# Narrow levels and diagonal of a gated linear attention multiplied in blocks of 32 keys and collected in a small tile of their own

## The chip, the cores and the metric

The kernel runs on one core of a Trainium2 chip. The metric is device time in microseconds (us) of one execution, as the median over several executions. Each executed kernel also has one profiled execution, which left a page of sums and a trace of every instruction; TensorE is called PE in it, its weight loads PEld, VectorE DVE, ScalarE ACT, GpSimd POOL, and SyncE, which starts the transfers, SP.

## What is computed

The program is one encoder block: an RMSNorm, a mix of two attention branches (stick-breaking attention and gated linear attention, GLA), and a gated MLP with a causal convolution, for 528 tokens of width 1024 in fp32 (16 learned tokens ahead of 512). The change touches only the GLA branch. It has four heads with keys of 128 channels and values of 256:

```python
def _gla(q, k, v, g):                     # S_t = diag(exp(g_t)) S_{t-1} + k_t^T v_t,  o_t = q_t S_t
    ...
        cum = jnp.cumsum(gi, axis=2)
        diff = cum[:, :, :, None, :] - cum[:, :, None, :, :]
        decay = jnp.exp(jnp.where(causal[None, None, :, :, None], diff, -jnp.inf))
        att = jnp.einsum('bhtd,bhsd,bhtsd->bhts', qi, ki, decay)
        o = jnp.einsum('bhts,bhsv->bhtv', att, vi) + jnp.einsum('bhtd,bhdv->bhtv', qi * jnp.exp(cum), state)
```

Inside a chunk, `att[t,s]` is a sum over channels d of q[t,d] k[s,d] exp(cum[t,d] - cum[s,d]) for s up to t. The decay depends on the channel, so the sum isn't one matrix product of q and k.

## The kernel before

The kernel works on chunks of 128 tokens: four, and a last one of 16 (`CHUNKS`). The function `gla` (L426) handles one head and builds the transposed attention of every chunk in one tile, `attT` (128 keys on the partitions, 528 queries along the row: chunk by chunk a block of 128 by 128, then 16 by 16).

To make matrix products of it, it splits the causal triangle of a chunk by levels. For a level lv, a chunk falls into pieces of 2 lv tokens; the queries of the second half of a piece see the keys of its first half. For these pairs exp(cum[t]-cum[s]) is split at the last key of the first half into a factor for the query and one for the key. `factors` (L441) makes them: DVE subtracts (`D`, L447), ACT takes two exponentials (L448, L449), DVE multiplies the keys (`kt`, L455) and the queries (`qt`, L456; only the query halves are kept, so a chunk has 64 columns at every level). `kt` is one of two buffers that are used in turn; where no keys of the level stand, it holds zeros or keys of an earlier level, whose products are unwanted. `D` has two buffers, too.

- The **wide levels** 64 and 32 multiply piece by piece (L466): 4 products of 64 keys by 64 queries, and 8 of 32 keys by 32. The products of level 32 go in turn to partitions 0 and 64 of the result `pl`. ACT copies the results to their places in `attT` (L469).
- The **narrow levels** 16, 8, 4, 2 and 1 (`LEVELS`, L470 on) multiply a whole chunk: 128 keys by the chunk's 64 queries (L476), four products for a level; levels 8 and less add one product of 16 keys by 8 queries for the last chunk (L478). Nearly all of a result is unwanted, since only pairs in the same piece count. A predicated copy of DVE (L481) writes those where a mask is set into `attT`: 128 x 256 elements for a level, and 16 x 8 for the tail. The masks `mk` (128 x 264 each) are made once, early in the program: POOL fills and selects 64 columns, and 8 for the tail (L341 to L354), and DVE copies the 64 columns three times.
- The **diagonal** (a token with itself; the factor is 1) is a product of k and q themselves, 128 x 128 for each chunk and 16 x 16 for the last (L437), into a tile `dg` from the pool of large results (`mmt`). A predicated copy of 128 x 512 (L439) puts the diagonal into `attT`, with a mask `mkd`.

Then `attT` is split into two tiles of fewer bits, `ah` and `al` (L484 to L486), which the output products read. `vt` (L497) are transposes of the values, `cum` (L430) the products that make the cumulated gates, `kdt` transposes of the keys for the state.

On PE an fp32 product is issued as two instructions, so that 4 products of L476 stand in the trace as x8. An fp32r product, as in the projections, is one.

The order of the work isn't the one in which the code stands. A scheduler plays the program through with estimated durations and writes one instruction stream for each engine. The heads run one after the other (L575 to L577): `gla(h)` and, beside it, projections that need nothing of it: the next head's `gla_proj` (keys, queries, values) and the gates `gr` of the same head (L555). Their products (L110: 128 x 128 weights by 256 or 258 columns) fill PE's stream between the small products of `gla`. They are called fills below. Their weights are brought by SP's queue, cast by ACT to `wh` (L89), and the rest `wl` is made by POOL (L90).

Small results lie in a pool `pss` (L65) with two tags of two buffers each: `pst(name)` takes tag "s", `pst(name, "z")` tag "z", which the levels use. Large results lie in `psm` with two buffers (`mmt`).

Of the kernel before, what the change touches and what calls it, by code (L numbers as in the profile page):

```python
# [9 lines left out]
F32 = mybir.dt.float32  # L10
F32R = mybir.dt.float32r
I32 = mybir.dt.int32
AF = mybir.ActivationFunctionType
ALU = mybir.AluOpType
PSUM = bass.MemoryType.PSUM

P = 128
# [4 lines left out]
T = NM + SEQ  # L22
# [18 lines left out]
CHUNKS = [(0, 128), (128, 128), (256, 128), (384, 128), (512, 16)]  # L41
# [3 lines left out]
CUT = (8, 16)  # L45
EARLY = 3
WIDE, LEVELS = (64, 32), (16, 8, 4, 2, 1)


@with_exitstack  # L50
def block_kernel(ctx: ExitStack, tc: tile.TileContext, x, meta_tokens, norm_mix_pre, w_in, w_gk_up, b_gk,
# [3 lines left out]
    pe, act, dve, pool, sp = nc.tensor, nc.scalar, nc.vector, nc.gpsimd, nc.sync  # L55

    x = x[0]
    out = out[0]
# [110 lines left out]
    ident = cst.tile([P, P], F32, name="ident")  # L169
# [45 lines left out]
    with tc.tile_pool(name="p0", bufs=2, side="right") as p0:  # L215
# [80 lines left out]
        for t, src in ((ghT, gla_head_norm[0]), (g1T, norm_mix_post[0]), (g2T, norm_ffn_pre[0]), (mT, meta_tokens[T0:, :])):  # L296
            n = src.shape[0] // P if len(src.shape) == 1 else src.shape[0] * KT
            r = p0.tile([n, P], F32, name=f"small{len(small)}", bufs=1)
# [34 lines left out]
    with ExitStack() as pgs:  # L333
        pgc = pgs.enter_context(tc.tile_pool(name="pgc", bufs=1))

        mk = {}
        mkd = pgc.tile([P, T], F32, name="mkd")
        for h in LEVELS:
            with tc.issue_after(low4.ins) if h < EASY else ExitStack():
                m = pgc.tile([P, 264], F32, name=f"mk{h}")  # L340
                pool.memset(m, 1.0)  # L341
                v3 = m[:, :64].rearrange("p (b i) -> p b i", i=h)
                pool.affine_select(out=v3, in_=v3, compare_op=ALU.is_ge, fill=0.0, base=0,
                                   pattern=[[-2 * h, 64 // h], [0, h]], channel_multiplier=1)
                pool.affine_select(out=v3, in_=v3, compare_op=ALU.is_ge, fill=0.0, base=h - 1,
                                   pattern=[[2 * h, 64 // h], [0, h]], channel_multiplier=-1)
                if h <= 8:
                    vt = m[:, 256:264].rearrange("p (b i) -> p b i", i=h)
                    pool.affine_select(out=vt, in_=vt, compare_op=ALU.is_ge, fill=0.0, base=0,
                                       pattern=[[-2 * h, 8 // h], [0, h]], channel_multiplier=1)  # L350
                    pool.affine_select(out=vt, in_=vt, compare_op=ALU.is_ge, fill=0.0, base=h - 1,
                                       pattern=[[2 * h, 8 // h], [0, h]], channel_multiplier=-1)
                with tc.issue_after(last_yg[0].ins):
                    dve.tensor_copy(m[:, 64:256].rearrange("p (c t) -> p c t", c=3), m[:, :64].unsqueeze(1).broadcast_to([P, 3, 64]))  # L354
                mk[h] = m
        with ExitStack():
            pool.memset(mkd, 1.0)
            pool.affine_select(out=mkd[:, 512:], in_=mkd[:, 512:], compare_op=ALU.is_equal, fill=0.0, base=0,
                               pattern=[[-1, 16]], channel_multiplier=1)
        with tc.issue_after(last_yg[0].ins):  # L360
            dve.tensor_copy(mkd[:, :512].rearrange("p (c t) -> p c t", c=4), ident.unsqueeze(1).broadcast_to([P, 4, P]))


        G = pgc.tile([P, 5, 512], F32, name="G")
# [61 lines left out]
        def gla(h, k, q, vT):  # L426

            pt = mmt(f"cum{h}")
# [3 lines left out]
            act.copy(cum, pt[:, :T])  # L432
            attT = pg.tile([P, T], F32, tag="attT", name=f"attT{h}", bufs=1)
            pool.memset(attT, 0.0)
            pt = mmt(f"dg{h}")
            for c, (t, n) in enumerate(CHUNKS):
                pe.matmul(pt[:n, t : t + n], k[:, t : t + n], q[:, t : t + n], start=True, stop=True)  # L437
            for rows, c in ((P, slice(0, 512)), (16, slice(512, T))):
                dve.copy_predicated(attT[:rows, c], mkd[:rows, c].bitcast(I32), pt[:rows, c])  # L439

            def factors(lv, n, kt):  # L441

# [27 lines left out]
            for i, lv in enumerate(LEVELS):  # L470
                n = 512 if lv >= 16 else T
                kt = kts[i % 2]
                qt = factors(lv, n, kt)
                pl = pst(f"pl{h}_{lv}", "z")
                for c in range(4):
                    pe.matmul(pl[:, c * 64 : c * 64 + 64], kt[:, c * P : (c + 1) * P], qt[:, c * 64 : c * 64 + 64], start=True, stop=True)  # L476
                if n == T:
                    pe.matmul(pl[:16, 256:264], kt[:, 512:T], qt[:, 256:264], start=True, stop=True)  # L478
                for rows, lo, hi in ((P, 0, 512), (16, 512, n)):
                    if lo < hi:  # L480
                        dve.copy_predicated(attT[:rows, lo:hi].rearrange("p (b l) -> p b l", l=2 * lv)[:, :, lv:],  # L481
                                            mk[lv][:rows, lo // 2 : hi // 2].rearrange("p (b l) -> p b l", l=lv).bitcast(I32),
                                            pl[:rows, lo // 2 : hi // 2].rearrange("p (b l) -> p b l", l=lv))
            ah = pg.tile([P, T], F32R, tag="ah", name=f"ah{h}", bufs=1)  # L484
            al = pg.tile([P, T], F32R, tag="al", name=f"al{h}", bufs=1)
            split(ah, al, attT)  # L486
# [685 lines left out]
```

## Time and profile before

| | us |
|---|---|
| three executions | 968.11, 969.35, 970.13 (median 969.35) |
| the profiled execution: its time | 969.08 |
| its span, first to last instruction | 967.3 |
| PE busy | 938.5, 97% of the span, 6588 matmuls |
| DVE busy | 661.5, 68% |
| ACT busy | 488.9, 51% |
| POOL busy | 357.6, 37% |
| mean granted clock of PE | 0.992 |

The profiled execution's time is 1.8 us longer than its span and 0.3 us below the median. In the trace each row of the timeline is one or several like instructions that stand next to each other: their start, the time from the first one's start to the last one's end, engine, line, operation, result and operands, shape and count. Products overlap in PE, so that the duration of a row is longer than the place it takes in PE's stream; that place is read from the starts of its neighbours.

### The profile page before, as it was taken

What the parts mean: (1) busy time and instruction counts of PE and PEld (TensorE: products, weight loads), DVE (VectorE), ACT (ScalarE), POOL (GpSimd) and SP (SyncE); (2) the same over time, 40 slices, a digit from 0 to 9 for tenths busy, and PEclk for the clock granted to TensorE, in tenths of its full rate; (3) what the DMA queues carried; (4) which work ended last, traced back from release to release, by engine and by line L of the source; (5) the groups of instructions that cost most, each with busy time, mean ns of one, the idle gap of its engine ahead of it and who ended that gap; (6) DMA issues with size and microseconds to landing.
All of it is one profiled execution on the core that took longest, in us unless ns stands there. A gap on an engine that the chain in (4) does not pass through costs nothing.

```text
span 967.3 us, 16621 instructions
## 1 busy us (share of the span) xinstructions
PE 938.5 (97%) x6588; PEld 866.3 (90%) x6588; DVE 661.5 (68%) x1110; ACT 488.9 (51%) x913; POOL 357.6 (37%) x268
## 2 busy tenths in 40 slices
PE   7999999999999998999999899999999999999996
PEld 7999999999999998999998678998999999988775
DVE  6675867767557877777858967554545554478897
ACT  5664554546377565665754235433333333355654
POOL 6523232222244554444545452444444444200200
PEclk9999999999999999999999999999999999999999
DMA  7122212221222321232213364233333233364923
GB/s 216 45 66 66 66 45 66 66 66 44 67 66 67 86 68 45 65 88 58 75 55 90 117 207 140 61 112 93 89 92 104 87 88 94 103 237 167 254 86 127
DMA packets 129727, 92.79 MB, mean 96 GB/s; under 512 B 4064, under 2 KB 114914, under 8 KB 129650
## 3 DMA queue, kind: packets, MB, share of 16 engines
q1 hardware_dynamic: 126178, 82.55, 28.8%
q0 software_dynamic: 1504, 2.88, 1.8%
q10 hardware_dynamic: 1968, 6.29, 1.8%
q8 instruction: 52, 0.85, 0.4%
q14 instruction: 25, 0.20, 0.1%
HBM read 87.52 MB, written 4.19 MB: 95 GB/s over the span
## 4 chain that ended last, share of the span: by engine, by line
PE 83%; DVE 10%; issue 2%; ACT 2%; POOL 2%; DMA 1%; DVEq 0%; ACTq 0%; POOLq 0%
PE pt_up L110 13%; PE ga L958 13%; PE pt_gr L110 5%; PE pt_gv L110 5%; PE pt_go L110 4%; PE pt_mg L110 4%; PE dA L1020 3%; PE pt_ms L110 3%; PE dD L1020 3%; PE pt_gk L110 2%; PE dB L1020 2%; PE wo L892 2%; PE pt_gq L110 2%; PE pt_sv L110 2%; PE pt_sk L110 2%
## 5 line engine op out<-in xcount | busy, mean ns | idle before, releaser
L90 POOL TENSOR_TENSOR wl_up<-raw_up,wh_up 128x1024 fp32r<-128x1024 f32 x22 | 53.0, 2409 | 68.3 <-ACT wh_up L89 68.3
L90 POOL TENSOR_TENSOR wl_ga<-raw_ga,wh_ga 128x1024 fp32r<-128x1024 f32 x22 | 55.2, 2509 | 56.6 <-ACT wh_ga L89 56.6
L110 PE MATMUL pt_up<-h2l,wh_up 128*128 128x256 f32 (+1 forms) x352 | 73.6, 283 | 0.3 <-DVE h2l L207 0.2
L110 PE MATMUL pt_up<-h2h,wh_up 128*128 128x256 f32 (+1 forms) x352 | 73.6, 283 | 0.2
L110 PE MATMUL pt_up<-h2h,wl_up 128*128 128x256 f32 (+1 forms) x352 | 73.3, 282 | 0.0
L958 PE MATMUL ga<-h2h,wl_ga 128*128 128x512 f32 (+1 forms) x192 | 72.2, 376 | 0.0
L958 PE MATMUL ga<-h2l,wh_ga 128*128 128x512 f32 (+1 forms) x192 | 72.2, 376 | 0.0
L958 PE MATMUL ga<-h2h,wh_ga 128*128 128x512 f32 (+1 forms) x192 | 72.0, 375 | 0.0
L89 ACT CAST wh_up<-raw_up 128x1024 fp32r<-128x1024 f32 x22 | 23.0, 1049 | 85.8 <-PE pt_up L110 76.2
L110 PEld LDWEIGHTS pt_up<-h2h,wh_up 128*128 128x128 f32 x352 | 56.9, 189 | 2.2 <-ACT h2h L206 0.5
L110 PEld LDWEIGHTS pt_up<-h2l,wh_up 128*128 128x128 f32 x352 | 55.5, 189 | 0.7 <-DVE h2l L207 0.7
L110 PEld LDWEIGHTS pt_up<-h2h,wl_up 128*128 128x128 f32 x352 | 55.3, 189 | 0.0
L958 PEld LDWEIGHTS ga<-h2h,wl_ga 128*128 128x128 f32 x192 | 36.2, 189 | 7.0
L949 DVE SCALAR_TENSOR_TENSOR cy<-pt_up,cw,cy 128x511 f32<-128x511 f32 (+1 forms) x22 | 16.4, 745 | 37.7 <-ACT cy L946 37.7
L958 PEld LDWEIGHTS ga<-h2l,wh_ga 128*128 128x128 f32 x192 | 36.2, 188 | 6.2
L958 PEld LDWEIGHTS ga<-h2h,wh_ga 128*128 128x128 f32 x192 | 36.2, 189 | 6.1
L949 DVE SCALAR_TENSOR_TENSOR yp<-pt_up,cw,yp 128x511 f32<-128x511 f32 (+1 forms) x22 | 16.4, 745 | 30.9 <-ACT yp L946 30.9
L89 ACT CAST wh_ga<-raw_ga 128x1024 fp32r<-128x1024 f32 x22 | 23.0, 1048 | 25.3 <-PE ga L958 24.8
L1048 POOL DMA_DIRECT2D tv<-in_w_ffn_down_dram x6 | 7.1, 1183 | 68.1 <-DVE wl_p L138 68.1
L90 POOL TENSOR_TENSOR wl_gr<-raw_gr,wh_gr 128x1024 fp32r<-128x1024 f32 x8 | 19.0, 2372 | 35.9 <-ACT wh_gr L89 33.1
L137 ACT CAST sh_p<-As 128x512 fp32r<-128x512 f32 (+1 forms) x30 | 17.4, 583 | 29.3 <-PE dB L1020 12.5
L90 POOL TENSOR_TENSOR wl_gv<-raw_gv,wh_gv 128x1024 fp32r<-128x1024 f32 x7 | 16.9, 2416 | 38.0 <-ACT wh_gv L89 38.0
(558 smaller groups left out, 3261.3 us busy)
## 6 DMA issues: line engine op xcount, KB each, us to landing
raw_up<-in_w_ffn_up_dram SPq DMA_DIRECT2D x22, 512.0 KB, 3.9
raw_ga<-in_w_ffn_gate_dram SPq DMA_DIRECT2D x22, 512.0 KB, 3.8
raw_t<-in_w_ffn_down_dram SPq DMA_DIRECT2D x10, 512.0 KB, 7.3
raw_gv<-in_w_in_dram SPq DMA_DIRECT2D x8, 512.0 KB, 3.9
raw_gr<-in_w_in_dram SPq DMA_DIRECT2D x8, 512.0 KB, 3.9
raw_mg<-in_w_in_dram SPq DMA_DIRECT2D x8, 512.0 KB, 3.9
raw_go<-in_w_gla_out_dram SPq DMA_DIRECT2D x8, 512.0 KB, 4.1
raw_ms<-in_w_in_dram SPq DMA_DIRECT2D x8, 512.0 KB, 4.0
```

The lines of the kernel that those rows point to most:

```text
L89: act.copy(hi_out, raw)
L90: lo_eng.tensor_tensor(out=lo_out, in0=raw, in1=f32(hi_out), op=ALU.subtract)
L110: pe.matmul(dst, a[:, k, :], b[:, k, lo:hi], start=n == 0, stop=n == len(steps) - 1)
L137: act.copy(hi, src)
L892: pe.matmul(d0[i], m[k][:, t], w, start=k == 0 and q == 0, stop=k == 7 and q == 2)
L949: dve.scalar_tensor_tensor(out=y[:, d:], in0=pt[:, : SEQ - d], scalar=c, in1=y[:, d:], op0=ALU.mult, op1=ALU.add)
L958: pe.matmul(pg_[:, lo:hi], a[:, k, :], b[:, k, lo:hi], start=lo == 0 and k == 0 and q == 0, stop=k == KT - 1 and q == 2, skip_group_check= ...
L1020: mm[i] = pe.matmul(dsts[i], a, b, start=first and k == 0 and j == 0, stop=last and k == NP - 1 and j == 2, skip_group_check=True)
L1048: return lambda n, q, nk: pool.dma_start(out=t[:, q : q + nk, :], in_=block(s, c, q, nk), accum_op=ALU.add)
```

## The change

The narrow levels and the diagonal multiply only blocks of 32 keys (`KB`), since a piece of level 16 has 32 tokens and no narrower level crosses such a block. A block of a narrow level has 16 queries (`QB`), one of the diagonal 32.

- A chunk has four blocks r = 0, 32, 64, 96; block r of chunk c is written to partitions r to r + 32 of the result, at columns 16 c (32 c for the diagonal). So a level has 16 products of 32 keys by 16 queries where it had 4 of 128 by 64. The tail products stay. The diagonal's result moves from the pool of large results to tag "s" of the small one.
- DVE's predicated copies now go into `near`, a tile of 128 x 5 x 32 that holds these blocks alone: 128 x 64 elements for a level, 128 x 128 for the diagonal. The masks shrink to 16 columns (32 for the diagonal) and are used for all chunks by a broadcast.
- After the last level ACT copies `near` to its four diagonal strips of `attT` (32 partitions each) and the tail, five copies a head, ahead of the cast to `ah`. POOL clears `near` once a head.
- The masks are made on 64 columns of a scratch tile with two buffers; POOL's selects for the tail and its work for `mkd` go away, and DVE makes the small masks by a sum (tensor_reduce) where it made copies.

```diff
+KB, QB = 32, 16
...
-                m = pgc.tile([P, 264], F32, name=f"mk{h}")
-                pool.memset(m, 1.0)
-                v3 = m[:, :64].rearrange("p (b i) -> p b i", i=h)
+                w = pgc.tile([P, 64], F32, tag="mw", name=f"mw{h}", bufs=2)
+                pool.memset(w, 1.0)
+                v3 = w.rearrange("p (b i) -> p b i", i=h)
...
-                if h <= 8:
-                    vt = m[:, 256:264].rearrange("p (b i) -> p b i", i=h)
...
+                m = pgc.tile([P, QB], F32, name=f"mk{h}")
                 with tc.issue_after(last_yg[0].ins):
-                    dve.tensor_copy(m[:, 64:256].rearrange("p (c t) -> p c t", c=3), m[:, :64].unsqueeze(1).broadcast_to([P, 3, 64]))
+                    dve.tensor_reduce(out=m, in_=w.rearrange("p (r i) -> p i r", i=QB), op=ALU.add, axis=mybir.AxisListType.X)
...
-            pool.memset(mkd, 1.0)
...
-            dve.tensor_copy(mkd[:, :512].rearrange("p (c t) -> p c t", c=4), ident.unsqueeze(1).broadcast_to([P, 4, P]))
+            dve.tensor_reduce(out=mkd, in_=ident.rearrange("p (r i) -> p i r", i=KB), op=ALU.add, axis=mybir.AxisListType.X)
...
-            pt = mmt(f"dg{h}")
-            for c, (t, n) in enumerate(CHUNKS):
-                pe.matmul(pt[:n, t : t + n], k[:, t : t + n], q[:, t : t + n], start=True, stop=True)
-            for rows, c in ((P, slice(0, 512)), (16, slice(512, T))):
-                dve.copy_predicated(attT[:rows, c], mkd[:rows, c].bitcast(I32), pt[:rows, c])
+
+            near = pg.tile([P, 5, KB], F32, tag="near", name=f"near{h}", bufs=1)
+            pool.memset(near, 0.0)
+            blocks = [(c, r, c * P + r, KB) for c in range(4) for r in range(0, P, KB)] + [(4, 0, 512, 16)]
+            pt = pst(f"dg{h}")
+            for c, r, t, n in blocks:
+                pe.matmul(pt[r : r + n, c * KB : c * KB + n], k[:, t : t + n], q[:, t : t + n], start=True, stop=True, skip_group_check=True)
+            for rows, c, n in ((P, slice(0, 4), KB), (16, slice(4, 5), 16)):
+                m = mkd[:rows, :n].bitcast(I32).unsqueeze(1)
+                dve.copy_predicated(near[:rows, c, :n], m.broadcast_to([rows, c.stop - c.start, n]),
+                                    pt[:rows, c.start * KB : c.stop * KB].rearrange("p (c t) -> p c t", t=KB)[:, :, :n])
...
-                for c in range(4):
-                    pe.matmul(pl[:, c * 64 : c * 64 + 64], kt[:, c * P : (c + 1) * P], qt[:, c * 64 : c * 64 + 64], start=True, stop=True)
-                if n == T:
-                    pe.matmul(pl[:16, 256:264], kt[:, 512:T], qt[:, 256:264], start=True, stop=True)
...
+                some = blocks if n == T else blocks[:16]
+                for c, r, t, kn in some:
+                    pe.matmul(pl[r : r + kn, c * QB : c * QB + kn // 2], kt[:, t : t + kn], qt[:, t // 2 : (t + kn) // 2],
+                              start=True, stop=True, skip_group_check=True)
...
+            for r in range(0, P, KB):
+                act.copy(av[r : r + KB, :, r : r + KB], near[r : r + KB, 0:4, :])
+            act.copy(attT[:16, 512:T], near[:16, 4, :16])
```

The scheduler also puts the streams in another order, since the small products are shorter to it. The following rows of the programs' order give line, operation, result, operands, shape of the result and count; numbers behind names count tiles. PE's stream at the beginning of the second head, where the diagonal stood between the transposes of the values, before:

```order
L430 MATMUL cum_1356<-ucum,G 128x128 x4
L430 MATMUL cum_1356<-ucum,G 128x16
L497 MATMUL vt_0_1484<-ident,gv_1243 128x128
L497 MATMUL vt_2_1491<-ident,gv_1243 128x128
L437 MATMUL dg_1366<-gq_1241,gk_1184 128x128 x4
L437 MATMUL dg_1366<-gq_1241,gk_1184 16x16
L497 MATMUL vt_0_1484<-ident,gv_1243 128x128 x3
L497 MATMUL vt_2_1491<-ident,gv_1243 128x128 x3
```

The same place after:

```order
L422 MATMUL cum_1430<-ucum,G 128x128 x4
L422 MATMUL cum_1430<-ucum,G 128x16
L433 MATMUL dg_1442<-gq_1315,gk_1258 32x32 x16
L433 MATMUL dg_1442<-gq_1315,gk_1258 16x16
L502 MATMUL vt_0_1637<-ident,gv_1317 128x128 x4
```

The diagonal now stands right behind `cum`, as 16 small products, and four transposes follow at once; the other four of `vt_2` stand 20 fills later. PE's stream around levels 16 and 8 of the second head before, with the fills `pt_gr` between the two:

```order
L476 MATMUL pl_16_1412<-qt_16_1409,kt_484 128x64 x4
L110 MATMUL pt_gr_1690<-hnl,wh_gr_1686 128x256
L110 MATMUL pt_gr_1690<-hnh,wl_gr_1687 128x258
L110 MATMUL pt_gr_1690<-hnh,wl_gr_1687 128x256
L110 MATMUL pt_gr_1690<-hnh,wh_gr_1686 128x258
L110 MATMUL pt_gr_1690<-hnh,wh_gr_1686 128x256
L110 MATMUL pt_gr_1690<-hnl,wh_gr_1686 128x258
L110 MATMUL pt_gr_1690<-hnl,wh_gr_1686 128x256
L476 MATMUL pl_8_1425<-qt_8_1422,kt_485 128x64 x4
L478 MATMUL pl_8_1425<-qt_8_1422,kt_485 16x8
```

After, from the last fill ahead of the two levels to the first behind them:

```order
L111 MATMUL pt_gr_1843<-hnh,wh_gr_1839 128x258
L475 MATMUL pl_16_1500<-qt_16_1497,kt_479 32x16 x16
L475 MATMUL pl_8_1525<-qt_8_1522,kt_480 32x16 x16
L475 MATMUL pl_8_1525<-qt_8_1522,kt_480 16x8
L111 MATMUL pt_gr_1843<-hnh,wh_gr_1839 128x256
```

Levels 16 and 8 stand side by side; so do 4 and 2, and the wide 64 and 32, while level 1 and the diagonal stand alone. DVE's stream of the second head from the differences of level 2 on, before:

```order
L447 TENSOR_TENSOR D_2_1448<-cum_1362 128x528
L481 COPY_PREDICATED attT_1364<-mk_335,pl_16_1412 128x16x16
L456 TENSOR_TENSOR qt_4_1437<-gq_1241,D_4_1433 128x264
L455 TENSOR_TENSOR kt_484<-gk_1184,D_4_1433 128x66x4
L447 TENSOR_TENSOR D_1_1463<-cum_1362 128x528
L481 COPY_PREDICATED attT_1364<-mk_340,pl_8_1425 128x32x8
L481 COPY_PREDICATED attT_1364<-mk_340,pl_8_1425 16x8
L455 TENSOR_TENSOR kt_485<-gk_1184,D_2_1448 128x132x2
L456 TENSOR_TENSOR qt_2_1452<-gq_1241,D_2_1448 128x264
```

And after:

```order
L445 TENSOR_TENSOR D_2_1572<-cum_1436 128x528
L482 COPY_PREDICATED near_1440<-mk_338,pl_16_1500 128x4x16
L453 TENSOR_TENSOR kt_479<-gk_1258,D_4_1545 128x66x4
L454 TENSOR_TENSOR qt_4_1549<-gq_1315,D_4_1545 128x264
L482 COPY_PREDICATED near_1440<-mk_344,pl_8_1525 128x8x8
L482 COPY_PREDICATED near_1440<-mk_344,pl_8_1525 16x8
L453 TENSOR_TENSOR kt_480<-gk_1258,D_2_1572 128x132x2
L454 TENSOR_TENSOR qt_2_1576<-gq_1315,D_2_1572 128x264
L445 TENSOR_TENSOR D_1_1599<-cum_1436 128x528
```

The predicated copies go to `near`, and the differences of level 1 have moved behind the factors of level 2.

More of the change, by code (lines that the diff above doesn't have):

```diff
@@ L336, in block_kernel @@
         mk = {}
-        mkd = pgc.tile([P, T], F32, name="mkd")
         for h in LEVELS:
             with tc.issue_after(low4.ins) if h < EASY else ExitStack():
-                m = pgc.tile([P, 264], F32, name=f"mk{h}")
-                pool.memset(m, 1.0)
-                v3 = m[:, :64].rearrange("p (b i) -> p b i", i=h)
+                w = pgc.tile([P, 64], F32, tag="mw", name=f"mw{h}", bufs=2)
+                pool.memset(w, 1.0)
+                v3 = w.rearrange("p (b i) -> p b i", i=h)
                 pool.affine_select(out=v3, in_=v3, compare_op=ALU.is_ge, fill=0.0, base=0,
@@ L346, in block_kernel @@
                                    pattern=[[2 * h, 64 // h], [0, h]], channel_multiplier=-1)
-                if h <= 8:
-                    vt = m[:, 256:264].rearrange("p (b i) -> p b i", i=h)
[L349 to L352, printed above, removed]
+                m = pgc.tile([P, QB], F32, name=f"mk{h}")
                 with tc.issue_after(last_yg[0].ins):
-                    dve.tensor_copy(m[:, 64:256].rearrange("p (c t) -> p c t", c=3), m[:, :64].unsqueeze(1).broadcast_to([P, 3, 64]))
+                    dve.tensor_reduce(out=m, in_=w.rearrange("p (r i) -> p i r", i=QB), op=ALU.add, axis=mybir.AxisListType.X)
                 mk[h] = m
-        with ExitStack():
-            pool.memset(mkd, 1.0)
-            pool.affine_select(out=mkd[:, 512:], in_=mkd[:, 512:], compare_op=ALU.is_equal, fill=0.0, base=0,
-                               pattern=[[-1, 16]], channel_multiplier=1)
+        mkd = pgc.tile([P, KB], F32, name="mkd")
         with tc.issue_after(last_yg[0].ins):
-            dve.tensor_copy(mkd[:, :512].rearrange("p (c t) -> p c t", c=4), ident.unsqueeze(1).broadcast_to([P, 4, P]))
+            dve.tensor_reduce(out=mkd, in_=ident.rearrange("p (r i) -> p i r", i=KB), op=ALU.add, axis=mybir.AxisListType.X)
         G = pgc.tile([P, 5, 512], F32, name="G")
@@ L474, in gla @@
                 pl = pst(f"pl{h}_{lv}", "z")
-                for c in range(4):
-                    pe.matmul(pl[:, c * 64 : c * 64 + 64], kt[:, c * P : (c + 1) * P], qt[:, c * 64 : c * 64 + 64], start=True, stop=True)
-                if n == T:
[L478 to L483, printed above, removed]
+                some = blocks if n == T else blocks[:16]
+                for c, r, t, kn in some:
+                    pe.matmul(pl[r : r + kn, c * QB : c * QB + kn // 2], kt[:, t : t + kn], qt[:, t // 2 : (t + kn) // 2],
+                              start=True, stop=True, skip_group_check=True)
+                for rows, c, kn in ((P, slice(0, 4), KB), (16, slice(4, 5), 16)):
+                    nc_, nb = c.stop - c.start, kn // (2 * lv)
+                    if c.start and n < T:
+                        continue
+                    m = mk[lv][:rows, : kn // 2].bitcast(I32).rearrange("p (b l) -> p b l", l=lv)
+                    dve.copy_predicated(near[:rows, c, :kn].rearrange("p c (b l) -> p c b l", l=2 * lv)[:, :, :, lv:],
+                                        m.unsqueeze(1).broadcast_to([rows, nc_, nb, lv]),
+                                        pl[:rows, c.start * QB : c.stop * QB].rearrange("p (c t) -> p c t", t=QB)[:, :, : kn // 2]
+                                        .rearrange("p c (b l) -> p c b l", l=lv))
+            for r in range(0, P, KB):
+                act.copy(av[r : r + KB, :, r : r + KB], near[r : r + KB, 0:4, :])
+            act.copy(attT[:16, 512:T], near[:16, 4, :16])
             ah = pg.tile([P, T], F32R, tag="ah", name=f"ah{h}", bufs=1)
```

## The prediction

> **What bounds the kernel now.** I read the page first: its span, the busy shares, the instruction queues (kind, packets, MB, share of 16 engines) and the chain that ended last.
>
> ```profile
> span 967.3 us, 16621 instructions
> ...
> PE 938.5 (97%) x6588; PEld 866.3 (90%) x6588; DVE 661.5 (68%) x1110; ACT 488.9 (51%) x913; POOL 357.6 (37%) x268
> ...
> q8 instruction: 52, 0.85, 0.4%
> ...
> PE 83%; DVE 10%; issue 2%; ACT 2%; POOL 2%; DMA 1%; DVEq 0%; ACTq 0%; POOLq 0%
> ```
>
> PE is busy 97% of the span and carries 83% of the chain. That alone doesn't say that a shorter product shortens the program, so the second view is busy time by stretches: one period of the heads (51 to 104 us), and the stretch that follows the heads. The first number behind the stretch is its length; then come the engines.
>
> ```profile
> core 0: us, PE busy (x) PEld busy (x) DVE busy (x) ACT busy (x) POOL busy (x), PEclk, DMA share, GB/s
> 51.00:104.00 53.00, 53.00 (x454) 51.22 (x453) 36.40 (x77) 28.02 (x62) 14.91 (x7) 1.00 0.23 62
> 264.00:300.00 36.00, 34.87 (x279) 33.57 (x278) 21.23 (x43) 22.89 (x48) 17.15 (x18) 1.00 0.25 66
> ```
>
> In the period of a head PE never idles (53.00 of 53.00) at full clock (1.00), DVE has 16.6 us to spare and ACT 25. Here what PE is spared comes off the end, as long as no other engine becomes late; PE has the fills to cover waits of the small products.
>
> **What the change removes on PE.** Since products overlap, I measure the place of a block from fill to fill, and take off the fills in it. The unit is a row of the critical chain (start, us, engine, result, line, count):
>
> ```profile
> 294.71 5.25 PE pt_mg L110 x44
> ```
>
> A fill takes 5.25 / 44 = 0.119 us. PE's timeline around levels 16 and 8 of the first head:
>
> ```profile
> 61.51 0.28 PE L110 MATMUL pt_gr<-hnl,wh_gr 128*128 128x258 f32 x1
> 61.63 1.00 PE L476 MATMUL pl<-qt,kt 128*128 128x64 f32 x8
> 62.44 0.37 PE L110 MATMUL pt_gr<-hnl,wh_gr 128*128 128x256 f32 x1
> 62.64 0.40 PE L110 MATMUL pt_gr<-hnh,wl_gr 128*128 128x258 f32 x2
> ...
> 63.35 1.00 PE L476 MATMUL pl<-qt,kt 128*128 128x64 f32 x8
> 64.28 0.21 PE L478 MATMUL pl<-qt,kt 128*16 128x8 f32 x2
> 64.42 0.51 PE L110 MATMUL pt_gr<-hnh,wl_gr 128*128 128x258 f32 x2
> 64.76 0.41 PE L110 MATMUL pt_gr<-hnh,wh_gr 128*128 128x258 f32 x2
> ```
>
> Level 16 takes from 61.63 to 62.64 with one fill in it: 1.01 - 0.12 = 0.89 us. Level 8 with its tail takes from 63.35 to 64.76 with two fills: 1.41 - 0.24 = 1.17. Levels 4, 2 and 1 have the same products as 8, so the five take 0.89 + 4 x 1.17 = 5.57 us a head. The diagonal, between transposes of the values:
>
> ```profile
> 104.66 1.30 PE L437 MATMUL dg<-gq,gk 128*128 128x128 f32 x10
> 105.90 0.87 PE L497 MATMUL vt<-ident,gv 128*128 128x128 f32 x6
> ```
>
> It takes 105.90 - 104.66 = 1.24. The change takes away 5.57 + 1.24 = 6.81 us of PE a head, 27.2 in all.
>
> **What it adds on PE.** A head gets four blocks: the diagonal, 16 + 8, 4 + 2, and 1. With two instructions for a product they have 34, 66, 68 and 34, so 202. No 32-key product with 16 queries is in the trace; the nearest is level 32 (32 keys, 32 queries). Its timeline, with level 64 (64 keys) ahead of it, and the group of its instructions with the mean of one:
>
> ```profile
> 57.25 0.68 PE L466 MATMUL pl<-qt,kt 128*64 128x64 f32 x8
> 57.85 0.39 PE L497 MATMUL vt<-ident,gv 128*16 128x128 f32 x2
> 58.00 0.48 PE L110 MATMUL pt_gr<-hnl,wh_gr 128*128 128x258 f32 x2
> 58.41 0.45 PE L466 MATMUL pl<-qt,kt 128*32 128x32 f32 x16
> 58.78 0.51 PE L110 MATMUL pt_gr<-hnh,wl_gr 128*128 128x258 f32 x2
> 59.12 0.40 PE L110 MATMUL pt_gr<-hnh,wh_gr 128*128 128x258 f32 x2
> ```
>
> ```profile
> L466 PE MATMUL pl<-qt,kt 128*32 128x32 f32 x64 | 1.8, 199 | 0.0
> ```
>
> From 58.00 to 59.12 there are four fills: 1.12 - 0.48 = 0.64 us is the most that the 16 instructions and both changes of shape take. The first fill pair, 58.00 to 58.41, is 0.17 longer than two fills; it holds the end of level 64's block as well, so I give half of that to it and take 0.56. The instructions themselves start (0.45 - 0.199) / 15 = 0.0167 us apart. So 0.56 - 16 x 0.0167 = 0.29 is what one block pays for the change into its shape and back.
>
> Now the choice that decides the size. At level 64 the starts are about 0.065 apart ((0.68 less some 0.23 for the last one) / 7), at 128 keys 0.105 ((1.00 less 0.27) / 7): they go with the number of keys, as if loading the weights set the pace. By that 32 keys would cost 0.033, and the trace shows half of it. What level 32 has and 64 has not is that its products go in turn to two places of the result, partitions 0 and 64: two of them load side by side. The new products go in turn to four places, 0, 32, 64 and 96. With four side by side an instruction takes 0.0083; if no more than two can, it stays at 0.0167. I take four: what the rows show is one pace for each place (0.033 at 32 keys), and no row shows that only two places can work at a time.
>
> - Four side by side: 4 x 0.29 + 202 x 0.0083 = 1.16 + 1.68 = 2.84 us a head. Spared: 6.81 - 2.84 = 3.97, in four heads **15.9 us**.
> - Two side by side: 1.16 + 202 x 0.0167 = 4.53. Spared 2.28, in four heads **9.1 us**.
>
> The bounds of the unknown price: from above, all of level 32's piece of the chain,
>
> ```profile
> 218.30 0.38 PE pl L466 x16
> ```
>
> 0.38 / 16 = 0.024 an instruction; from below 0.0083 with half the switching price, 0.145 instead of 0.29, which would spare another 0.58 a head, 2.3 in all. The other shifts on PE (diagonal ahead of the transposes, wide levels side by side with a transpose apart) leave the number of changes of shape as it was: nothing.
>
> A rule of the Trainium skill speaks against the choice. Its page "TensorE: Matmul & The Clock Gate", section "Wait — 56ns, not 53.3ns?", says that matmuls never start less than about 25 ns apart, however few columns they have. By it the 202 instructions would take 5.05 us and a head 6.21, 0.60 less than now: 2.4 us in all. Level 32's instructions, 0.0167 apart, are below that floor already.
>
> **Beside PE.** DVE's copies shrink; the groups of the large ones of before, and of a strip copy by ACT as the new ones are, over the four heads:
>
> ```profile
> L481 DVE COPY_PREDICATED attT<-mk,pl 128x256 f32<-128x256 int32 x20 | 11.2, 561 | 6.7 <-PE pl L478 3.5 <-PE pl L476 3.2
> ...
> L469 ACT COPY attT<-pl 32x128 f32<-32x128 f32 x8 | 2.0, 247 | 0.0
> ```
>
> A copy of a level now has a quarter of the elements (64 of 256 a partition), so up to three quarters of the 11.2 go, on an engine off the path. ACT gets five copies a head, 5 x 0.247 = 1.2 us, on an engine that is busy 28 of 53. They stand between the last level and the cast to `ah`, which the output products need; 28 fills and the transposes of the keys stand between level 1 and those, over 3 us (28 x 0.119). If that cover were gone, it would be 1.2 us a head. Clearing `near` is one small step of POOL, a head ahead. SP's queue keeps its order. All this costs nothing.
>
> What can become late is DVE. Heads get shorter by 4 us, and levels now come in pairs: the second of a pair must have its factors when the first starts. DVE has been caught behind POOL:
>
> ```profile
> 61.69 2.50 POOL L90 TENSOR_TENSOR wl_gk<-raw_gk,wh_gk 128x1024 fp32r<-128x1024 f32 x1 [8.39 <-ACT wh_gk L89]
> ...
> 63.09 1.40 DVE L456 TENSOR_TENSOR qt<-gq,D 128x264 f32<-128x264 f32 x1
> ...
> 64.41 0.42 DVE L455 TENSOR_TENSOR kt<-gk,D 128x264 f32<-128x264 f32 x1
> ```
>
> A product that takes 0.42 took 1.40, and ended only when POOL's subtraction did. I put 0.2 us a head on PE waits from such a catch, a fifth of the 0.98 that one costs: **0.8 us** against the change. The ends are 0 and 0.98 x 4 = 3.9.
>
> At the start POOL makes fewer masks, which run beside the first steps of the norm:
>
> ```profile
> 6.94 0.25 POOL L345 TENSOR_SCALAR_AFFINE_SELECT mk<-mk 128x64 f32<-128x64 f32 x1
> 7.03 0.72 DVE L212 TENSOR_SCALAR drin<-ident,a_in 128x128 f32<-128x128 f32 x1
> ```
>
> That DVE step stands ahead of the first transposes of the input. Without POOL's work beside it, it may take about half: **0.3 us** gained, between 0.6 gained and, since the order there shifts as well, 0.3 lost.
>
> **The sum.** The profiled execution's time is 969.08, 0.27 below the median of the runs, 969.35. 969.08 - 15.9 + 0.8 - 0.3 = **953.7 us**.
>
> **The rivals.**
> - Two side by side: all as above with 9.1; heads get shorter by 2.3 us only, so DVE has more time, and I leave its 0.8 out: 969.08 - 9.1 - 0.3 = 959.7. For it: it is exactly what level 32 shows. Against: level 32 offers only two places. Chance 0.22.
> - DVE becomes late: in each head one step is caught as the 1.40 one, 3.9 in place of 0.8 plus 0.9 for the pairs it holds up: 953.7 + 4.0 = 957.7. For it: POOL makes a remainder of 2.5 us for every tile of weights, and a catch is a matter of a microsecond. Against: PE's stream before absorbs them with fills. Chance 0.08.
> - A floor of starts at 0.024: 1.16 + 202 x 0.024 = 6.0, spared 0.8 a head: 969.08 - 3.2 - 0.3 = 965.6. For it: the chain's row, if the switching is no part of it. Against: the 0.0167. Chance 0.06. (With the 25 ns of the Trainium skill's page named above it would be 969.08 - 2.4 - 0.3 = 966.4.)
> - PE's instructions come late, slower than before: short products use up the program faster than before. A block of queue q8 has 0.85 MB / 52 = 16 KB; PE and PEld together have 13176 instructions, 0.85 MB / 13176 = 65 B each at most. A block of 68 products with their loads is 136 instructions, 8.8 KB, in under a microsecond, while a block took 0.4% x 16 x 967 / 52 = 1.2 us of one DMA engine's time. If each of 16 blocks waits for one landing, it costs 19.2 of what was spared 15.9: 953.7 + 19.2 = 972.9. It decides from 15.4 / 16 = 0.96 us a block on. Against: the block of 16 at 58.41 shows no such wait, and "issue" is 2% of the chain. Chance 0.04.
> - The gain doesn't come (the scheduler's new stream gives it back in waits of PE elsewhere): 968 to 971, chance 0.04.
>
> **How the numbers follow.** The forecast has 0.52; 0.04 is left for faster than it. Its own range is 951.5 (half the switching price) to 956.5 (0.98 in three of four heads). With the two next cases, up to 962, the range 951.5 to 962.0 leaves out the floor, the late instructions, no gain, and the 0.04 below: about 0.18. A measurement of this kernel tells 0.2%, 1.9 us, from no change. Faster by more: the forecast, the first two rivals, what is below, and the floor: 0.92. The case without gain lies around 0.2% on both sides, and I give 0.03 of its 0.04 to the same; with the late instructions slower has 0.05.
>
> **What would show it.** In the timeline after, a level's 32 instructions take 0.0083 x 32 + 0.2, about 0.45 to 0.5 us from first start to last end, with four side by side, and 0.7 with two. PE stays without waits between 51 and 250 us; if DVE is late, the row of the second level of a pair shows an idle time ended by `qt` or `kt`. The first transposes (L264) start some 0.3 earlier. Heads that get shorter by less than 2 us would prove the forecast wrong, and so would idle time of PE of over 1 us a head.

## The result and the profile after

The changed kernel takes 954.43 us (median of 4, 953.63 to 956.72) beside 968.87 for the kernel before (median of 4): a ratio of 0.9849, with a 95% interval of 0.9828 to 0.9870. In the two later comparisons it had 0.9860 (0.9838 to 0.9881) and 0.9832 (0.9818 to 0.9847). Forecast were 953.7 us.

The profiled execution took 956.72 us and is the longest of the four. Its page:

```profile
span 954.8 us, 17806 instructions
...
PE 926.2 (97%) x7164; PEld 854.3 (89%) x7164; DVE 655.4 (69%) x1110; ACT 492.3 (52%) x933; POOL 360.7 (38%) x262
...
q8 instruction: 56, 0.92, 0.4%
...
PE 82%; DVE 10%; issue 3%; ACT 3%; POOL 2%; DMA 1%; DVEq 0%; ACTq 0%; POOLq 0%
```

PE issues 576 more matmuls and is busy 12 us less. It is still the engine of the chain. One group of products marks the heads: the cumulated gates open each head, and this row gives the start of the first and the last of all four heads' products. Before, and after:

```profile
L430 PE MATMUL cum<-ucum,G x40: 257/275/278, 49.8 to 210.6; 128*128 128x128 f32 x32, 16*128 16x16 f32 x8
```

```profile
L422 PE MATMUL cum<-ucum,G x40: 257/275/278, 50.7 to 199.8; 128*128 128x128 f32 x32, 16*128 16x16 f32 x8
```

From the first of these products to the last, which holds three distances of heads, it was 160.8 us and is 149.1: 3.9 us less for each. From start to start a head took 53.25 us and takes 49.35; that is called the heads' distance below. The forecast was 3.97 less 0.2 for waits, 3.77. The small blocks in PE's timeline of the first head after:

```profile
52.00 0.48 PE L433 MATMUL dg<-gq,gk 128*32 128x32 f32 x34
52.41 0.66 PE L502 MATMUL vt<-ident,gv 128*128 128x128 f32 x4
...
61.66 0.40 PE L111 MATMUL pt_gr<-hnh,wl_gr 128*128 128x258 f32 x2
61.99 0.75 PE L475 MATMUL pl<-qt,kt 128*32 128x16 f32 x66
62.67 0.51 PE L111 MATMUL pt_gr<-hnh,wh_gr 128*128 128x258 f32 x2
...
65.39 0.28 PE L111 MATMUL pt_gr<-hnh,wl_gr 128*128 128x258 f32 x1
65.61 0.82 PE L475 MATMUL pl<-qt,kt 128*32 128x16 f32 x68
66.35 0.39 PE L111 MATMUL pt_gr<-hnh,wl_gr 128*128 128x256 f32 x1
```

From fill to fill, without the fills: the diagonal takes 0.41 us, levels 16 and 8 take 1.01 - 0.24 = 0.77, levels 4 and 2 take 0.96 - 0.12 = 0.84. Single starts of level 16 stand in fours: three 6 to 7 ns apart, then 12 until the next four, so that four take 0.032 us and an instruction 0.008. In level 8, right behind it, the steps are uneven (1 to 2 and 14 to 17 ns in turn), but four take 0.032 again. That is the case of four places side by side. The waits of PE in the four heads (40 to 252 us) are one row:

```profile
PE pl L475 <- DVE qt L454: 0.4, 1, 0.4
```

### The profile page after: what moved, and what is told of

It is laid out like the page before. It is cut to its first block, busy times and chain, and to the rows that moved or that the text cites. A ratio compares the mean times of both kernels' runs of the same rounds, so it can differ in the third digit from the quotient of the medians.

```text
span 954.8 us, 17806 instructions
## 1 busy us (share of the span) xinstructions
PE 926.2 (97%) x7164; PEld 854.3 (89%) x7164; DVE 655.4 (69%) x1110; ACT 492.3 (52%) x933; POOL 360.7 (38%) x262
## 4 chain that ended last, share of the span: by engine, by line
PE 82%; DVE 10%; issue 3%; ACT 3%; POOL 2%; DMA 1%; DVEq 0%; ACTq 0%; POOLq 0%
PE pt_up L111 13%; PE ga L963 13%; PE pt_gv L111 5%; PE pt_gr L111 5%; PE pt_go L111 4%; PE pt_mg L111 4%; PE dA L1025 3%; PE dD L1025 3%; PE pt_gk L111 3%; PE pt_sv L111 2%; PE pt_gq L111 2%; PE dB L1025 2%; PE pt_ms L111 2%; PE wo L897 2%; PE pt_sk L111 2%
## 5 line engine op out<-in xcount | busy, mean ns | idle before, releaser
L111 PE MATMUL pt_gr<-hnh,wh_gr 128*128 128x258 f32 (+1 forms) x128 | 28.2, 294 | 0.0
```

What stands on the lines that cost most here:

```text
L111: pe.matmul(dst, a[:, k, :], b[:, k, lo:hi], start=n == 0, stop=n == len(steps) - 1)
```

## The experiments

The theory that I took from it: a place (32 partitions of the result) takes a 32-key instruction every 0.032 us, and the four places work at the same time. The rival that the result leaves is that the products are fast because they are small, wherever they write. I tell the heads' distance for each kernel, since it doesn't hang on the start or the tail of the program.

**The order of the places.** In two kernels the blocks alone are reordered; PE's stream is the same but for the order inside a block.

```diff
-            blocks = [(c, r, c * P + r, KB) for c in range(4) for r in range(0, P, KB)] + [(4, 0, 512, 16)]
+            blocks = [(c, r, c * P + r, KB) for r in range(0, P, KB) for c in range(4)] + [(4, 0, 512, 16)]                              # same_place
+            blocks = [(c, r, c * P + r, KB) for pair in ((0, 64), (32, 96)) for c in range(4) for r in pair] + [(4, 0, 512, 16)]         # two_places
```

> The same products in another order: all four chunks of place 0, then of 32, 64, 96, so that four products in a row (eight instructions) write to one place. Theory (four places load side by side, each place takes a product instruction every 0.032 us): 192 instructions a head go from 0.008 to 0.032 apart, 192 x 4 x 0.024 = 18 us more than the changed kernel, about 972 to 973; a block of 66 takes 2.1 us in place of 0.5. Rival (the gain comes from the products being small, wherever they write): no change, 954 to 955. If PE looks further ahead than eight instructions, something between.

> The same products in another order: in turn to places 0 and 64, then in turn to 32 and 96. Theory: 192 instructions a head go from 0.008 to 0.016 apart, 192 x 4 x 0.008 = 6 us more than the changed kernel, about 960 to 961, which is what the prediction's first rival had. Rival (small products, wherever they write): 954 to 955.

> The changed kernel once more, as the measure for the others and to see what varies by itself. Both theories: 953.5 to 956. In its first trace the first transposes of the input start 0.112 us apart before and 0.213 after, and level products of the stick-breaking branch behind an idle of 0.9 us are slow for some 3.6 us in place of 2.1. If that is chance and not the change, it is gone or elsewhere in this trace.

Measured, beside 969.95 us for the kernel before in the same rounds: the changed kernel again 956.30, same_place 961.88 (ratio 0.9919, 0.9899 to 0.9940), two_places 955.85 (0.9862, 0.9837 to 0.9887). The heads' row and the block of levels 16 and 8 in same_place:

```profile
L422 PE MATMUL cum<-ucum,G x40: 257/275/278, 50.5 to 205.9; 128*128 128x128 f32 x32, 16*128 16x16 f32 x8
```

```profile
61.93 0.40 PE L111 MATMUL pt_gr<-hnh,wl_gr 128*128 128x258 f32 x2
62.27 1.50 PE L475 MATMUL pl<-qt,kt 128*32 128x16 f32 x66
63.69 0.51 PE L111 MATMUL pt_gr<-hnh,wh_gr 128*128 128x258 f32 x2
```

And the same block in two_places:

```profile
60.25 0.40 PE L111 MATMUL pt_gr<-hnh,wl_gr 128*128 128x258 f32 x2
60.58 0.92 PE L475 MATMUL pl<-qt,kt 128*32 128x16 f32 x66
61.42 0.51 PE L111 MATMUL pt_gr<-hnh,wh_gr 128*128 128x258 f32 x2
```

With the place kept for eight instructions the block takes 1.76 - 0.24 = 1.52 us in place of 0.77, and the heads' distance is 51.4 in place of 49.35 us. So the place matters, and "small wherever they write" falls. But the theory asked for 18 / 4 = 4.6 us a head, and only 2.05 came. The single starts of the block show where: it opens with 0.052, 0.032, 0.031, 0.032 us between starts, which is one place's pace, and then goes on in pairs (0.006, 0.026, 0.026, 0.005, 0.027, ...), 0.019 on average. The trace doesn't name the place of a start. I read the pairs so that PE had the next place's instructions at work while the first place still had some to go, further ahead than the theory had it; no run tests that reading. In two_places this goes further: 0.93 us for the block, and a heads' distance of 49.6, so hardly a third of a microsecond a head is lost. So same_place came out between the two expectations, which was named there for PE looking further ahead than eight instructions, and two_places came out near its rival (954 to 955) and not at the theory's 960 to 961. The pace of one place (0.032) and the overlap of several places stand; the order must be quite bad before it costs much.

**Twice the products.**

```diff
-            for c, r, t, n in blocks:
+            for c, r, t, n in blocks + blocks:
...
-                for c, r, t, kn in some:
+                for c, r, t, kn in some + some:
```

> Every product of the narrow levels and the diagonal is issued twice, the second over the first, so that the output stays; the number of blocks stays, too. Theory (0.008 for an instruction and the rest for the change into the shape and back): 192 x 4 x 0.008 = 6 us for the blocks, and 2 to 3 us for the second products of 16 keys, which go to one place: 961 to 964. Rival (0.0167 for an instruction and cheaper changes of shape): 13 us and the 2 to 3, 968 to 971.

Measured: 967.46 us (ratio 0.9972, 0.9951 to 0.9993), between the two expectations, so that the time fits neither. The blocks decide; here are levels 16 and 8 in the first head:

```profile
59.87 0.28 PE L111 MATMUL pt_gr<-hnl,wh_gr 128*128 128x258 f32 x1
60.08 1.34 PE L475 MATMUL pl<-qt,kt 128*32 128x16 f32 x132
61.36 0.39 PE L111 MATMUL pt_gr<-hnl,wh_gr 128*128 128x256 f32 x1
```

They take 1.49 - 0.12 = 1.37 us in place of 0.77, so 0.60 for 66 more instructions, 0.009 each: the price of the theory and not the 0.0167 of the rival. At 0.009 the 202 more instructions of a head cost 1.8 us, 7.3 in four heads, of the 11.2 us between this kernel and the changed one in the same rounds. Some of the rest is in new waits of PE in the heads:

```profile
PE pl L475 <- issue: 2.7, 2, 2.4
PE pl L475 <- DVE qt L454: 2.5, 4, 0.7
```

DVE's factors came late, by 0.7 us at most in a head. In the third head PE also stood for 2.36 us in the middle of a doubled block and waited for nothing that the profile shows, and behind that, from 172.80 to 176.20 us, the granted clock was 0.51. A wait in that place is what the prediction's slower rival (instructions that come late) would have; whether it is that isn't shown. It happened once, with twice the instructions, and in none of the three traces of the changed kernel.

**Parts of the change.** In levels_only the diagonal's products are those of before, in a large result:

```diff
-            pt = pst(f"dg{h}")
-            for c, r, t, n in blocks:
-                pe.matmul(pt[r : r + n, c * KB : c * KB + n], k[:, t : t + n], q[:, t : t + n], start=True, stop=True, skip_group_check=True)
+            pt = mmt(f"dg{h}")
+            for c, (t, n) in enumerate(CHUNKS):
+                pe.matmul(pt[:n, t : t + n], k[:, t : t + n], q[:, t : t + n], start=True, stop=True)
...
```

> The narrow levels as in the changed kernel, the diagonal's products as before (128 x 128 in a large result); DVE copies the diagonal from there to the small tile in four strips and the tail. By the prediction's steps the levels give 5.57 - 1.16 x 3/4 - 168 x 0.008 = 3.36 us a head and the diagonal 1.24 - 0.29 - 34 x 0.008 = 0.68: heads' distance 53.25 - 3.4 = 49.9 us, the time 2.7 us over the changed kernel, 957 to 959. Rival (what was gained came from the diagonal's new place ahead of the transposes and from the large result it no longer holds): distance above 51.

Measured: 960.44 us (ratio 0.9898, 0.9883 to 0.9914), heads 51.0 us apart. That is a microsecond a head more than forecast. The waits of PE tell where it went:

```profile
PE pl L476 <- ACT D L448: 2.4, 3, 0.8
PE pl L476 <- DVE kt L454: 1.1, 1, 1.1
```

0.8 to 1.1 us a head are waits for a level's factors; in this kernel DVE has five small copies for the diagonal, and in three of the heads the scheduler pairs levels 8 and 4, and 2 and 1. The sign that was named for the rival, a distance above 51, did come, by 0.04 us. The blocks speak against the rival all the same. Levels 16 and 8 of the first head:

```profile
61.15 0.28 PE L111 MATMUL pt_gr<-hnh,wl_gr 128*128 128x258 f32 x1
61.36 0.75 PE L476 MATMUL pl<-qt,kt 128*32 128x16 f32 x66
62.04 0.39 PE L111 MATMUL pt_gr<-hnh,wl_gr 128*128 128x256 f32 x1
```

They take 0.89 - 0.12 = 0.77 us, as in the changed kernel, with the diagonal in its old place and form. Taking the waits off gives a distance of 50.2, by which the levels bring 3.1 us of the 3.9 and the diagonal the rest; that is a subtraction and no measured time.

**The price of a block.** One kernel has a block less, one has no products of 16 keys.

```diff
+                if lv == 16:
+                    with tc.issue_after(mm.ins):      # dg_with16: mm is the last product of level 16
+                        pt = pst(f"dg{h}")
...
-    blocks = [...] + [(4, 0, 512, 16)]
+    blocks = [...]                                    # no_tail
```

> The changed kernel with the diagonal's products put behind those of level 16 in PE's stream, in one block with 16 and 8, so that a head has three blocks in place of four. Theory (each block pays about 0.25 us for the change into the shape and back): the heads' distance falls from 49.35 to 49.1 us, 1 us in all. Rival (the change of shape is paid at each product of 16 keys, of which the block now has two): 49.35, no change.

> The changed kernel without the products and copies for the last chunk of 16 tokens (narrow levels and diagonal), so those pairs are left out of the attention. Theory (the change into the shape and back costs 0.25 us a block, whatever stands last in it): the five products of 16 keys spare their starts alone, about 0.04 us each, 0.2 us a head: distance of the heads 49.1 to 49.2. Rival (the change back is paid at the product of 16 keys): each of the four blocks that ends in one spares over 0.1, 0.5 to 0.7 a head: 48.6 to 48.9.

dg_with16 took 956.65 us (ratio 0.9854, 0.9837 to 0.9870), with heads 50.2 us apart: slower a head by 0.9. Its waits:

```profile
PE vt L503 <- DVE vl L139: 2.7, 4, 0.7
```

0.7 us in each head: the transposes of the values now wait for DVE's split of the ones before. With those taken off, 49.5 remains, so that nothing of the 0.25 is seen in the distance. In PE's stream the joint block of 100 instructions takes 1.02 us from its first start to the next product, where its parts took 0.41 and 0.68 in the changed kernel: 0.07 less. (The diagonal's own block holds only 0.41 - 34 x 0.008 = 0.14 us beyond its instructions.) So the 0.25 isn't borne out for this block; whether a product of 16 keys inside the block pays again isn't settled by this kernel. no_tail took 953.93 us in its one run; its second and third distance are 49.07 and 49.09 us (in the first PE waited 0.68 for DVE's `kd`), 0.3 less than in the changed kernel. Only a part of that is the price of the five products of 16 keys. From first start to the next fill, levels 16 and 8 fall from 0.68 to 0.67 us and level 1 from 0.40 to 0.38, but levels 4 and 2 from 0.99 and 0.96 us (second and third head) to 0.74 and 0.70, since PE pauses less inside that block for late factors. So the five products themselves cost about 0.1 us a head, under the theory's 0.2 and far under the 0.5 to 0.7 of the rival: most of the price of a block is paid without them.

**The start.**

```diff
+                    xk = pgc.tile([P, 264], F32, tag="mx", name=f"mx{h}", bufs=1)
+                    pool.memset(xk, 1.0)
+                    vt = xk[:, 256:264].rearrange("p (b i) -> p b i", i=h)
...
```

> The changed kernel with part of POOL's early mask work put back beside it (fills of 264 columns and the selects for the tail, on a tile that nobody reads). By the prediction's start term the first transposes of the input start 0.3 us or more later than the 7.1 to 7.2 us of the changed kernel, towards the 7.8 of before. Rival (they start when the input has landed, or DVE's steps do, whatever POOL does): 7.1 to 7.2. The heads' distance stays 49.35.

> The kernel before once more, for its start: in its first trace the first transposes of the input start at 7.81 us, at full speed, and the cumulated gates begin at 49.8. By the prediction's start term (the masks' work of POOL holds up DVE) the transposes start at 7.8 again, against 7.1 to 7.3 in every trace with the small masks. Rival (chance of the start): 7.1 to 7.3, or full and half speed change from trace to trace here as well.

masks_kept took 955.68 us in its one run, before_again 971.34. PE's timeline of the first transposes of the input, in the kernel before, once more in before_again, in the changed kernel's first trace, and in masks_kept:

```profile
7.81 2.05 PE L264 MATMUL tp<-drin,xt 128*128 128x128 f32 x16 [1.16 <-DVE v_in L122]
```

```profile
7.82 3.43 PE L264 MATMUL tp<-drin,xt 128*128 128x128 f32 x16 [1.17 <-DVE v_in L122]
```

```profile
7.23 3.78 PE L265 MATMUL tp<-drin,xt 128*128 128x128 f32 x16 [0.57 <-DVE drin L213]
```

```profile
7.09 3.79 PE L265 MATMUL tp<-drin,xt 128*128 128x128 f32 x16 [0.43 <-DVE drin L213]
```

Two things are in these rows. The transposes start at 7.8 us in both traces of the kernel before and at 7.3 or earlier in the twelve others: 0.5 to 0.7 us gained (1.1 in twice), about twice the forecast. masks_kept doesn't give it back, though its POOL does selects for the tail again, one of them beside the DVE step ahead of the transposes (`drin`). That step takes 0.29 us there, as in all twelve, and 0.72 and 0.73 in the kernel before. So selects and fills as such didn't hold DVE up. In the two traces of before POOL's cast `tri` runs beside `drin` (7.15 us); in the twelve others it is done by 6.0. Whether that is the cause isn't shown.

And 16 transposes take 2.05 us or 3.4 to 3.8: in 5 of 14 traces, one of them of the kernel before, most of them start 0.213 us apart and not 0.112. The trace's record of the granted clock begins, with full speed, only at 10.6 to 11.4 us in these five, and at 7.1 us or earlier in the nine others. (The view by stretches shows 1.00 there in any case, since it takes off only what the record holds.) That is half speed at the start, as chance has it from execution to execution. It costs 1.3 to 1.5 us by the first product of the cumulated gates: that stands at 50.7, 50.5 and 49.2 us in the three traces of the changed kernel, at 49.8 and 51.1 in the two of the kernel before.

**The wide levels as well.** If four places are better than one or two, levels 64 and 32 can have them:

```diff
-                for b in range(4 * 64 // lv):
-                    c, r = divmod(b * lv, 64)
-                    pe.matmul(pl[2 * r : 2 * r + lv, c * lv : c * lv + lv], kt[:, 2 * lv * b : 2 * lv * b + lv],
-                              qt[:, b * lv : b * lv + lv], start=True, stop=True, skip_group_check=True)
+                for c in range(4):
+                    o = (lv if lv == 64 else 32) * (c % 2)
+                    for s in range(0, 64, 32):
+                        t, b = (s, c) if lv == 64 else (2 * s, 2 * c + s // 32)
+                        row = o + s if lv == 64 else o + 2 * s
+                        pe.matmul(pl[row : row + 32, c // 2 * lv : c // 2 * lv + lv], kt[:, c * P + t : c * P + t + 32],
+                                  qt[:, b * lv : b * lv + lv], start=True, stop=True, skip_group_check=True)
...
```

> The changed kernel, with the wide levels on four places as well: level 64 as eight products of 32 keys by 64 queries (even chunks to places 0 and 32, odd ones to 64 and 96), level 32 with odd chunks at 32 and 96; ACT copies each level in twice as many, smaller copies. Theory (a place takes an instruction every 0.032 us, four places side by side): level 64 goes from 8 x 0.058 = 0.47 to 16 x 0.008 = 0.13 us, level 32 from 16 x 0.0167 = 0.27 to 0.13, together 0.48 a head: the distance of the heads falls from 49.35 to 48.9 us, 1.9 us in all, about 953. Rival (the look ahead already lays the two levels over each other, or ACT's three more copies hold the heads up): 49.35, 954 to 956.

> Once more the kernel with the wide levels on four places as well, now on the same chip and in the same rounds as the changed kernel itself. Theory (0.3 to 0.5 us less a head): 1.1 to 2 us below the changed kernel beside it. Rival (the difference seen before was the chip): within 0.5 us of it.

> The changed kernel beside it: heads 49.35 us apart whatever the start does; 953.5 to 956.5. If the half speed of the first transposes is chance, cumulated gates begin at 49.2 us in some traces of this kernel and at 50.6 in others.

Measured: 953.17 us at first (ratio 0.9818, 0.9802 to 0.9835), then 952.65 (0.9820, 0.9807 to 0.9834) beside 954.59 for the changed kernel in the same rounds (0.9832, 0.9818 to 0.9847). The two levels in the changed kernel, second head, and in wide_four_b, first head:

```profile
107.12 0.28 PE L111 MATMUL pt_gr<-hnh,wh_gr 128*128 128x258 f32 x1
107.33 1.05 PE L464 MATMUL pl<-qt,kt 128*64 128x64 f32 x24
108.32 0.39 PE L111 MATMUL pt_gr<-hnh,wh_gr 128*128 128x256 f32 x1
108.54 0.40 PE L111 MATMUL pt_gr<-hnl,wh_gr 128*128 128x258 f32 x2
```

```profile
56.19 0.40 PE L111 MATMUL pt_gr<-hnh,wl_gr 128*128 128x258 f32 x2
56.52 0.56 PE L467 MATMUL pl<-qt,kt 128*32 128x64 f32 x32
57.00 0.50 PE L111 MATMUL pt_gr<-hnh,wh_gr 128*128 128x258 f32 x2
57.34 0.40 PE L111 MATMUL pt_gr<-hnl,wh_gr 128*128 128x258 f32 x2
```

From 107.12 to 108.32 with one fill it was 1.20 - 0.12 = 1.08 us; now 0.81 - 0.24 = 0.57, with more instructions: 0.51 less, near the 0.48 that the theory gave. The heads' distance fell by less, from 49.35 to 49.06 us. Counted from start to start, the second head gives back 0.2 us at the cumulated gates, which products of another tile now cut in two, 0.2 in the fills and 0.1 in the output products; why the last two got longer wasn't found out. In time the two medians are 1.9 us apart, with intervals that overlap: the gain is shown in the rows, and is probable, not sure, in the time. It is the shortest kernel of this study.

## Why the prediction was right

- **What bounds the kernel.** PE's spared time came off the end: three heads gave 11.7 us, and the time fell by 13.7 to 15.6 us in three comparisons. By the rows four heads at 3.9 and 0.6 at the start make 16.2. The medians hold the chance of the clock as well (below). Two traces that are alike in it, before_again and after_again, both with half speed at the start and 10.2 us at half clock later on, have spans of 969.6 and 952.8 us, 16.8 apart.
- **The size of a block.** The forecast had 2.84 us a head with four places side by side; the first head shows 0.41 + 0.77 + 0.84 and for level 1, from the same view,

```profile
69.00 0.41 PE L111 MATMUL pt_gk<-hnl,wh_gk 128*128 128x272 f32 x2
69.33 0.47 PE L475 MATMUL pl<-qt,kt 128*32 128x16 f32 x34
69.73 0.51 PE L111 MATMUL pt_gk<-hnh,wl_gk 128*128 128x272 f32 x2
```

  0.73 - 0.24 = 0.49: 2.51 in all. (The row's 0.47 us is the 0.45 to 0.5 that the prediction named for four places.) The 0.0083 an instruction was right (0.008, and 0.009 with the products of 16 keys in twice); the change of shape was put too high, at 0.29, where 2.51 - 202 x 0.008 = 0.9 for four blocks leaves 0.22. By these blocks a head spares 6.81 - 2.51 = 4.3 us, 0.4 more than the distances show. The next point is 0.15 of that in the three distances; the rest wasn't found out. The choice of four places rested on a pace by the number of keys that the prediction read from whole rows. The single starts bear it out: 0.111 us at 128 keys, 0.058 at 64 (the prediction's 0.065 holds the longer first step) and 0.032 at 32 in one place. That more than two places work at once was a choice that no row could show then; it is what came true.
- **DVE behind POOL.** The 0.8 us for four heads was nearly met. A product of DVE beside POOL's subtraction takes 1.95 or 1.96 us in place of 0.42 in each of the four heads, and ends 0.3 us after POOL's step. (So did the 1.40 us of the prediction's row, which says that it ended with it.) In the second head level 2's queries came after PE had begun the block:

```profile
111.07 2.87 POOL L91 TENSOR_TENSOR wl_gk<-raw_gk,wh_gk 128x1024 fp32r<-128x1024 f32 x1 [7.61 <-ACT wh_gk L90]
...
112.27 1.96 DVE L453 TENSOR_TENSOR kt<-gk,D 128x264 f32<-128x264 f32 x1
...
115.00 1.06 PE L475 MATMUL pl<-qt,kt 128*32 128x16 f32 x68
...
115.05 0.42 DVE L454 TENSOR_TENSOR qt<-gq,D 128x264 f32<-128x264 f32 x1
```

  From its first start to the next fill this block takes 0.99 us, in place of 0.75 in the first head; in the third head it is 0.96, in the fourth 1.20 with a wait of 0.36. Together that is 0.9. The mechanism is the one that was named, but that a fifth of a catch would reach PE was a guess that fitted by luck, and no run takes POOL's step away: that the catch made the queries late is read from the rows.
- **Beside PE.** The copies cost nothing, as said: ACT's five took 1.4 us a head in place of 1.2 (0.292 each for the strips), and PE waits for none of them between 40 and 252 us. DVE's large copies went from 561 to 244 ns.
- **The start** was mis-sized, 0.6 for 0.3, at the end of its range, and the reason given for it (POOL's mask work beside `drin`) isn't borne out by masks_kept.
- **The rivals.** Two places side by side (959.7) is refuted by the single starts in fours and by the blocks of 0.8 us. Of DVE becoming late the catches came, in every head, but PE lost 0.9 us to them and not the 4.8 of that rival. The floor near 0.025 us, which the Trainium skill states in "TensorE: Matmul & The Clock Gate", section "Wait — 56ns, not 53.3ns?", doesn't hold for products on different places: they start 0.006 to 0.007 us apart. A wait such as instructions that come late would make was seen once, in twice, and not here.
- **The range.** The upper end of the prediction's own range, 956.5, doesn't come out of its words: 0.98 us in three of four heads in place of the 0.8 gives 955.8. Nothing hangs on it.

The profiled execution lies 3 us above the forecast for another reason, for the larger part: half speed at the start (1.4 us), and once more behind the heads. The granted clock of that stretch, with what the engines did in it:

```profile
256.00:259.00 3.00, 2.75 (x17) 2.45 (x15) 1.34 (x4) 2.48 (x4) 0.92 (x1) 0.69 0.00 0
```

The stretch has a granted clock of 0.69 (the column ahead of the last two). In the changed kernel's second trace it is 1.00:

```profile
256.00:259.00 3.00, 2.75 (x24) 2.48 (x23) 1.08 (x3) 2.20 (x4) 1.20 (x1) 1.00 0.00 0
```

So neither belongs to the change: before_again has half speed at the start, too. Such stretches of 3.4 or 6.8 us at half clock stand in every trace, between the heads and the end (the last microseconds, without products, aside): 10.2 us in both traces of the kernel before, 13.6, 10.2 and 20.4 in the three of the changed one. From the start of the fourth head to the end the changed kernel takes 756.1, 754.3 and 759.3 us, more where there is more half clock.

## What to carry to other kernels

In these traces small fp32 products are paid by the number of weight columns (0.111, 0.058 and 0.032 us an instruction for 128, 64 and 32, one after the other), and by where their results go: products with 32 weight columns whose results go in turn to partitions 0, 32, 64 and 96 run four at a time (0.008), and a mask over a full 128 x 128 product pays for columns that nobody wants. Before such a change, look for one product in the trace that already alternates between two places, and price the new ones by it; measure from fill to fill, since the rows of overlapping products are longer than the place they take. Then ask what the shorter stage lets become late: here it was a step of DVE behind POOL, at 0.2 us a head.

## What had not been expected of the hardware

- Products to different places seem to overlap even where four products in a row (eight instructions) go to the same one: starts 0.019 us apart, where one place alone takes 0.032 and four in turn 0.008. With pairs of places in turn the loss is a third of a microsecond a head.
- The first 16 transposes take 2.05 us in 9 traces and 3.4 to 3.8 in 5, of either kernel, after the same warm-up products: this program carries some 1.4 us of chance from its first 12 us, and more from the stretches at half clock later on.
- A wait of PE of 2.36 us that nothing in the profile ends, in the kernel with 404 more products (twice), and half clock for 3.4 us behind it.
